# The first mixer's chunk products in diagonal 64x64 tiles, with the whole 64x64 inverse applied during preparation

## The chip, the cores and the metric

The kernel runs on one core of a Trainium2 chip, as one program. The metric is the device time of the program in microseconds (us). Three runs of the kernel before took 3040.48 us in the median (3040.01 to 3050.44). A core has TensorE (PE, matrix products into the accumulator memory PSUM), VectorE (DVE), ScalarE (ACT), GpSimd (POOL) and SyncE (SP, which only issues transfers), and each of these works through its own list of instructions in order.

## The reference

It is one transformer block over 2048 tokens of width 1024: a norm, an input projection `h @ w_in`, two mixers (`hgrn2_mixer`, `rwkv7_mixer`), gates and projections back, and a mixture of experts. The change touches the RWKV mixer, here called the first mixer. For each of its 8 heads it carries a 64x64 state through time:

```
sa = einsum('bhij,bhj->bhi', state, a_t)          # a_t = -kk_t
state = (state * w_t[:, :, None, :] + sa[..., None] * b_t[:, :, None, :]
         + v_t[..., None] * k_t[:, :, None, :])   # b_t = kk_t * a
y_t = einsum('bhij,bhj->bhi', state, r_t)
```

followed by a group norm per head, a bonus term (r * k * r_k summed, times v) and a gate.

## The kernel before, in words

The tokens are worked in 16 blocks of 128 (`TB`), a block in two chunks of 64 tokens. The eight heads lie as four pairs: pair `m` has its two heads on partitions 0 to 63 and 64 to 127.

Inside a chunk the recurrence is solved by products. With the decay taken into the vectors, a chunk needs A and R (`AR`, columns 0 to 63 and 64 to 127), B and K (`BK`), the masked products of these (`Gc`), and U, the solution of a unit triangular system of 64 steps whose right side is A times the state plus a product of `Gc` with the values. Then the state gets B and K times U and the values, and the output is R times the state plus `Gc` times U and the values.

`rw_prep(k, b)` prepares block b without the state. It loads the projected columns (`rwin`, L156), computes tanh, sums, exponentials and the lora products (L173), the norms of the keys (L196, with `iv` as their inverse), the eight products `Gc` in four groups (L224, with L226 as scaling, mask and copy out of PSUM), and sends the 32x32 corners through DRAM (`Nd`) so that all heads' small triangles lie on partitions (`Nl`). A substitution of 31 steps on DVE (L243, L244) inverts each 32x32 triangle; the result goes through DRAM again (`Pd`) and comes back as `Pa` (L251). Transposes give `BT` (L258, L260) and the values `UV` (L268, L272), and the last product is the bonus, `bon` (L279, L280).

`rw_chain(k, b, prep)` runs the two chunks with the state `Sbd` (a 128x128 matrix for each pair, with zeros off the diagonal). Since the inverse is there only for the 32x32 halves, a chunk goes through four dependent steps with a copy on ACT after each: right side of the first half, its solution, the second half's right side, its solution. All its products stand at L296, the one-line helper `mm`. `rw_out` norms, gates and stores a block's output.

What sets the order. The main loop goes over four groups of 512 tokens and issues for each block in turn: the preparation of block b+1, some tiles of input projection, the chain of block b, more projection tiles, the second mixer (`hg_block`), more projection. A planner then orders each engine's list: it takes the instruction that stands earliest in the code among those whose inputs and buffers it expects to be ready, with some blocks of `hg_block` moved forward (`hp`, `HP`). So projection tiles (L770 to L772) fill PE where the mixers wait. From the end of the fourth group on, `mixed` (L853 to L855) takes this place.

Buffers are handed out by name. A name has as many slots as its `bufs`, one where none is given, and the planner gives the slots of a name to its tiles in the order of the code. For this case two names matter: `rp` in PSUM, one slot, through which every product of the preparation goes, and `rwin` in SBUF, one slot.

Of the kernel before, what the change touches and what calls it, by code (L numbers as in the profile page):

```python
# [17 lines left out]
TB = 128  # L18
# [71 lines left out]
def rw_consts(k, I):  # L90
# [4 lines left out]
    k.hind = cp.tile([128, 2], FP, name="hind")  # L95
    nc.gpsimd.memset(k.hind, 0.0)
    nc.gpsimd.memset(k.hind[0:64, 0:1], 1.0)
    nc.gpsimd.memset(k.hind[64:128, 1:2], 1.0)
# [38 lines left out]
    k.iv = [cp.tile([128, TB // 64, 8], FP, name=f"iv{j}") for j in range(2)]  # L137
    for t in k.iv:
        nc.vector.memset(t, 1.0)
    k.Sbd = cp.tile([128, 4, 128], FP, name="Sbd")  # L140
    nc.vector.memset(k.Sbd, 0.0)
# [7 lines left out]
def rw_prep(k, b):  # L149
# [49 lines left out]
    nc.vector.tensor_scalar(iv[0:64], nrm, 1e-24, 2.0, op0=OP.max, op1=OP.mult)  # L199
    nc.vector.reciprocal(iv[0:64], iv[0:64])  # L200
# [17 lines left out]
    for c in range(NC):  # L218
        Gc = w2p.tile([128, 2, 4, 128], FP, name="Gc", bufs=4)
        for hp in range(2):  # L220
            pt = ps.tile([128, 4, 128], FP, name="rp")
            h = slice(hp * 64, hp * 64 + 64)
            for m in range(4):
                nc.tensor.matmul(pt[:, m], BK[h, m, c, :], AR[h, m, c, :], start=(m == 0), stop=True, skip_group_check=True)  # L224
            for m in range(4):
                nc.vector.scalar_tensor_tensor(Gc[:, hp, m], pt[:, m], iv[:, c, 2 * m + hp:2 * m + hp + 1], k.gmask, op0=OP.mult, op1=OP.mult)  # L226
        for hf in range(2):
            q = slice(hf * 32, hf * 32 + 32)
            nc.sync.dma_start(Nd[hf, c * 8:(c + 1) * 8].rearrange("x s t -> s x t"), Gc[q, :, :, q].rearrange("p a m t -> p (a m) t"))
        Gs.append(Gc)  # L230
# [18 lines left out]
    Pa = w2p.tile([64, NC * 8, 32], FP, name="Pa", bufs=2)  # L249
    for hf in range(2):  # L250
        nc.sync.dma_start(Pa[hf * 32:hf * 32 + 32], Pd[hf].rearrange("x s t -> s x t"))  # L251


    BT = []
    for c in range(NC):
        pt = ps.tile([128, 512], FP, name="rp")
        for m in range(4):
            nc.tensor.transpose(pt[:, m * 128:(m + 1) * 128], BK[:, m, c, :], k.ident)  # L258
        t = w2p.tile([128, 4, 128], FP, name="BT", bufs=4)
        nc.vector.tensor_tensor(t.rearrange("p m (h x) -> p (m h) x", h=2), pt.rearrange("p (h x) -> p h x", h=8),  # L260
                                iv[:, c, :, None].to_broadcast([128, 8, 64]), OP.mult)
        BT.append(t)

    UV = []
    for c2 in range(NC // 2):
        pt = ps.tile([128, 512], FP, name="rp")
        for m in range(4):
            nc.tensor.transpose(pt[:, m * 128:(m + 1) * 128], v_[:, m, c2 * 128:(c2 + 1) * 128], k.ident)  # L268
        for j in range(2):
            u = w2p.tile([128, 512], FP, name="UV", bufs=4)  # L270
            nc.gpsimd.memset(u[0:64], 0.0)
            nc.scalar.copy(u[64:128], pt[j * 64:j * 64 + 64])  # L272
            UV.append(u)

# [6 lines left out]
    return AR, Gs, Pa, BT, UV, GE, bon, sY  # L281


def rw_chain(k, b, prep):
# [4 lines left out]
    AR, Gs, Pa, BT, UV, GE, bon, sY = prep  # L289
    Yb = None  # L290
    for c in range(NC):
        Gc, u = Gs[c], UV[c]
        xy = ps.tile([128, 512], FP, name="xy")
        px = ps.tile([128, 512], FP, name="px")
        R = wk.tile([64, 512], FP, name="R")
        mm = lambda *a_, **kw: nc.tensor.matmul(*a_, skip_group_check=True, **kw)  # L296
        hs = [(h, h // 2, h % 2, slice(h * 64, h * 64 + 64)) for h in range(8)]
        for m in range(4):
            mm(xy[:, m * 128:(m + 1) * 128], AR[:, m, c, :], k.Sbd[:, m, :], start=(m == 0), stop=False)
        for h, m, hp, sl in hs:  # L300
            mm(xy[0:64, sl], Gc[:, hp, m, 0:64], u[:, sl], start=False, stop=False)
        nc.scalar.copy(R[0:32], xy[0:32])
        for h, m, hp, sl in hs:
            mm(px[0:32, sl], Pa[0:32, c * 8 + hp * 4 + m, :], R[0:32, sl], start=(h == 0), stop=True)
        nc.scalar.copy(u[0:32], px[0:32])
        for h, m, hp, sl in hs:
            mm(xy[32:64, sl], Gc[0:32, hp, m, 32:64], u[0:32, sl], start=False, stop=False)
        nc.scalar.copy(R[32:64], xy[32:64])
        for h, m, hp, sl in hs:
            mm(px[32:64, sl], Pa[32:64, c * 8 + hp * 4 + m, :], R[32:64, sl], start=(h == 0), stop=True)  # L310
        nc.scalar.copy(u[32:64], px[32:64])
        sp = ps.tile([128, 4, 128], FP, name="px")
        for m in range(4):
# [1206 lines left out]
```

## Time and profile before

| | |
|---|---|
| median of three runs | 3040.48 us |
| the profiled execution | 3035.84 us |
| its span, first to last instruction | 3034.1 us |
| PE busy in the span | 2770.9 us |
| DVE, ACT, POOL busy in the span | 2141.7, 1453.0, 1381.0 us |

The profile is of one execution. An engine's busy time is the time in which at least one of its instructions runs; a matmul is shown from its start to a modelled end, so that neighbours overlap. The mixers run from some 140 us to 1970 us, the experts from about 2200 on.

### The profile page before, as it was taken

The numbers are of one execution on the slowest core, as the hardware profiler recorded it, in microseconds if no ns is written. First come the engines' busy times: TensorE is split into PE (matmuls) and PEld (weight loads), VectorE is DVE, ScalarE is ACT, GpSimd is POOL, SyncE is SP. The second block draws the span as 40 slices with busy tenths as digits, with TensorE's granted clock in tenths as the row PEclk, the third lists the DMA queues.
The fourth block names the chain that finished last, engine by engine and source line by source line (L and its number), as shares of the span: only waits on it lengthen the run. The fifth ranks groups of instructions, "written<-read, shape, count | busy, mean of one in ns | idle before, by whom it ended". The sixth has DMA issues, their size and how long they took to land. (4 is left out here: it accounts for less than half of the span.)

```text
span 3034.1 us, 46921 instructions
## 1 busy us (share of the span) xinstructions
PE 2770.9 (91%) x15562; PEld 2268.7 (75%) x15562; DVE 2141.7 (71%) x4010; ACT 1453.0 (48%) x2507; POOL 1381.0 (46%) x1416
## 2 busy tenths in 40 slices
PE   5999999999999999989999988989987999999993
PEld 5877778778777878778777877868875777777772
DVE  5265787675687667787658778546574698998884
ACT  4334444534444534444434454442233576676763
POOL 3435555655555655565564566663333112221112
PEclk7999999999989999999999998999988999999996
DMA  7565344564444654454453554686456799999996
GB/s 222 161 201 148 100 133 120 151 183 134 105 133 114 181 154 134 113 152 133 131 136 101 150 160 148 203 298 212 152 189 175 260 368 364 363 352 362 361 315 249
DMA packets 569571, 593.16 MB, mean 195 GB/s; under 512 B 113841, under 2 KB 441521, under 8 KB 569218
## 3 DMA queue, kind: packets, MB, share of 16 engines
q1 hardware_dynamic: 556978, 555.11, 57.4%
q0 software_dynamic: 11088, 29.60, 4.2%
q10 hardware_dynamic: 1152, 4.19, 0.4%
q8 instruction: 165, 2.70, 0.4%
q14 instruction: 188, 1.54, 0.2%
HBM read 476.87 MB, written 118.77 MB: 196 GB/s over the span
## 5 line engine op out<-in xcount | busy, mean ns | idle before, releaser
L765 POOL TENSOR_TENSOR wlo<-wraw,whi 128x512 fp32r<-128x512 f32 x368 | 490.9, 1337 | 429.0 <-ACT whi L764 369.4
L770 PE MATMUL mm<-hThi,whi 128*128 128x512 f32 x1472 | 597.3, 406 | 14.8 <-ACT hThi L667 11.9
L772 PE MATMUL mm<-hThi,wlo 128*128 128x512 f32 x1472 | 592.7, 403 | 9.2 <-POOL wlo L765 8.9
L771 PE MATMUL mm<-hTlo,whi 128*128 128x512 f32 x1472 | 592.0, 402 | 1.8 <-DVE hTlo L668 1.8
L1203 DVE TENSOR_TENSOR wlo<-raw,whi 128x1024 fp32r<-128x1024 f32 x404 | 484.1, 1255 | 44.4 <-ACT whi L1202 21.8
L1202 ACT CAST whi<-raw 128x1024 fp32r<-128x1024 f32 x408 | 405.1, 1057 | 209.2 <-PE U L928 51.7
L764 ACT CAST whi<-wraw 128x512 fp32r<-128x512 f32 x368 | 225.9, 616 | 308.6 <-PE mm L771 192.3
L770 PEld LDWEIGHTS mm<-hThi,whi 128*128 128x128 f32 x1472 | 283.2, 192 | 82.3 <-ACT hThi L667 12.4
L772 PEld LDWEIGHTS mm<-hThi,wlo 128*128 128x128 f32 x1472 | 282.4, 192 | 73.0 <-POOL wlo L765 13.8
L771 PEld LDWEIGHTS mm<-hTlo,whi 128*128 128x128 f32 x1472 | 282.9, 192 | 60.7 <-DVE hTlo L668 2.8
L1291 POOL DMA_INDIRECT X<-y,lists x33 | 72.2, 2189 | 489.7 <-DVE y L1289 445.3
L243 DVE TENSOR_TENSOR pr<-Pl,Nl 128x2 f32<-128x2 f32 (+30 forms) x496 | 260.3, 525 | 12.2
L451 POOL TENSOR_TENSOR Xq<-h,kf 128x256 f32<-128x256 f32 x96 | 81.5, 849 | 114.3 <-ACT h L448 71.0
L244 DVE TENSOR_REDUCE Pl<-pr 128x1 f32<-128x2 f32 (+30 forms) x496 | 123.7, 249 | 11.5
L447 ACT ACTIVATE h<-h 128x256 f32<-128x256 f32 x96 | 40.4, 420 | 161.7 <-DVE h L446 158.0
L296 PE MATMUL xy<-UV,Gc 128*64 128x64 f32 (+1 forms) x1536 | 114.6, 224 | 0.0
L1233 PE MATMUL G<-whi,xh 128*128 128x512 f32 x256 | 104.9, 410 | 9.5 <-PEq L1364 8.3
L853 PE MATMUL mm<-hThi,whi 128*128 128x512 f32 x256 | 105.0, 413 | 9.3 <-ACT hThi L667 9.3
L296 PEld LDWEIGHTS xy<-UV,Gc 128*64 128x64 f32 (+1 forms) x1536 | 96.6, 128 | 17.6 <-issue 6.1
L854 PE MATMUL mm<-hTlo,whi 128*128 128x512 f32 x256 | 105.3, 411 | 3.3 <-DVE hTlo L668 3.3
L849 POOL TENSOR_TENSOR wlo<-wraw,whi 128x512 fp32r<-128x512 f32 x64 | 89.0, 1393 | 40.3 <-ACT whi L848 28.5
L226 DVE SCALAR_TENSOR_TENSOR Gc<-rp,iv,gmask 128x128 f32<-128x128 f32 x256 | 71.7, 342 | 46.3 <-PE rp L224 45.8
(492 smaller groups left out, 6184.8 us busy)
## 6 DMA issues: line engine op xcount, KB each, us to landing
wraw<-in_w_in_dram SPq DMA_DIRECT2D x368, 256.0 KB
raw<-in_exp_w_gate_dram SPq DMA_DIRECT2D x126, 512.0 KB
raw<-in_exp_w_up_dram SPq DMA_DIRECT2D x126, 512.0 KB
raw<-in_exp_w_down_dram SPq DMA_DIRECT2D x124, 512.0 KB
HGP<-ev SPq DMA_DIRECT2D x64, 256.0 KB
xin<-in_ada_w_dram SPq DMA_DIRECT2D x32, 512.0 KB
hgin<-HGP SPq DMA_DIRECT2D x16, 1024.0 KB
GTP<-ev SPq DMA_DIRECT2D x64, 256.0 KB
```

The source lines that it names most:

```text
L243: nc.vector.tensor_tensor(pv, Pl[:, :ni, :ns], Nl[:, :ns, t_][:, None, :].to_broadcast([128, ni, ns]), OP.mult)
L244: nc.vector.tensor_reduce(Pl[:, :ni, t_], pv, AX.X, OP.add)
L296: mm = lambda *a_, **kw: nc.tensor.matmul(*a_, skip_group_check=True, **kw)
L764: nc.scalar.copy(whi, raw)
L765: nc.gpsimd.tensor_tensor(wlo, raw, whi.bitcast(FP), OP.subtract)
L770: nc.tensor.matmul(pt, whi[:, kk % 4], hi[kk // 2][:, kk % 2], start=(kk == 0), stop=False)
L771: nc.tensor.matmul(pt, whi[:, kk % 4], lo[kk // 2][:, kk % 2], start=False, stop=False)
L772: nc.tensor.matmul(pt, wlo[:, kk % 4], hi[kk // 2][:, kk % 2], start=False, stop=(kk == 7))
L853: nc.tensor.matmul(pt, whi[:, kk], hi[o // 2][:, o % 2], start=(kk == 0), stop=False)
L854: nc.tensor.matmul(pt, whi[:, kk], lo[o // 2][:, o % 2], start=False, stop=False)
L1202: s.nc.scalar.copy(hi, raw)
L1203: eng.tensor_tensor(lo, raw, hi.bitcast(FP), OP.subtract)
```

## The change

The two heads of a pair get products of their own, on rows and columns 0 to 63 and 64 to 127 of the array, issued in turns. The state becomes `Sst`, 64x64 for each head. The two 32x32 inverses are joined to the whole 64x64 inverse (`PT`) in the preparation, which multiplies A by it (back into `AR`) and the values' part of the right side (into the second half of `UV`). The chain then needs one addition where it had four dependent steps. Transposes become products with a 64x64 identity. Cut to its core:

```diff
@@ rw_prep
-    nrm = pt[0:64, 0, 0:8 * NC].rearrange("p (c h) -> p c h", c=NC)
+    nrm = pt[:, 0, 0:4 * NC].rearrange("p (c m) -> p c m", c=NC)
+    mm = lambda *a_, **kw: nc.tensor.matmul(*a_, skip_group_check=True, **kw)
     for c in range(NC):
         for m in range(4):
-            nc.tensor.matmul(nrm[:, c, 2 * m:2 * m + 2], sq[:, m, c], k.hind, start=(c + m == 0), stop=True,
-                             skip_group_check=True)
+            for h in HEADS:
+                mm(nrm[h, c, m:m + 1], sq[h, m, c], k.ones[h, 0:1], start=(c + m == 0), stop=True)
...
-        for hp in range(2):
+        for w in range(2):
             pt = ps.tile([128, 4, 128], FP, name="rp")
-            h = slice(hp * 64, hp * 64 + 64)
             for m in range(4):
-                nc.tensor.matmul(pt[:, m], BK[h, m, c, :], AR[h, m, c, :], start=(m == 0), stop=True, skip_group_check=True)
+                for h in HEADS:
+                    mm(pt[h, m], BK[h, m, c, w * 64:w * 64 + 64], AR[h, m, c, :], start=(m == 0), stop=True)
+            if w:
+                nc.vector.tensor_tensor(Gc[:, 1], pt, k.gmask[:, None, :].to_broadcast([128, 4, 128]), OP.mult)
+                continue
             for m in range(4):
-                nc.vector.scalar_tensor_tensor(Gc[:, hp, m], pt[:, m], iv[:, c, 2 * m + hp:2 * m + hp + 1], k.gmask, op0=OP.mult, op1=OP.mult)
-        for hf in range(2):
-            q = slice(hf * 32, hf * 32 + 32)
-            nc.sync.dma_start(Nd[hf, c * 8:(c + 1) * 8].rearrange("x s t -> s x t"), Gc[q, :, :, q].rearrange("p a m t -> p (a m) t"))
+                nc.vector.scalar_tensor_tensor(Gc[:, 0, m], pt[:, m], iv[:, c, m:m + 1], k.gmask, op0=OP.mult, op1=OP.mult)
+            for hp in range(2):
+                for hf in range(2):
+                    q = slice(hp * 64 + hf * 32, hp * 64 + hf * 32 + 32)
+                    x = hp * NC * 4 + c * 4
+                    nc.sync.dma_start(Nd[hf, x:x + 4].rearrange("x s t -> s x t"), Gc[q, 0, :, hf * 32:hf * 32 + 32])
...
+    PT = k.PT[b % 2]            # four loads from Pd, two as Pa before
+    for c in range(NC):
+        ab, kv = (ps.tile([128, 512], FP, name="rp") for _ in range(2))
+        for m in range(4):
+            for h in HEADS:
+                mm(ab[h, m * 64:m * 64 + 64], AR[h, m, c, 0:64], k.ident[h, h], start=(m == 0), stop=True)
+        ...                     # B into ab; K and v into kv; copies to at, t and u
+        pt = ps.tile([128, 512], FP, name="rp")
+        for m in range(4):
+            for h in HEADS:
+                mm(pt[h, m * 64:m * 64 + 64], Gs[c][h, 1, m, 0:64], u[h, m * 64:m * 64 + 64], start=(m == 0), stop=True)
+        nc.scalar.copy(u[:, 256:512], pt[:, 0:256])
+    first, second = (tuple(slice(h.start + o, h.start + o + 32) for h in HEADS) for o in (0, 32))
+    P1T = wk.tile([128, NI * 32], FP, name="pr").rearrange("p (x j) -> p x j", j=32)
+    nc.vector.transpose(P1T, PT[:, :, 0:32])
+    pt = ps.tile([128, 512], FP, name="rp")
+    for x in range(NC * 4):
+        for a1, a2 in zip(first, second):
+            mm(off(pt)[a2, x], Gs[x // 4][a1, 0, x % 4, 32:64], P1T[a1, x], start=(x == 0), stop=True)
+    Q = wk.tile([128, NI, 32], FP, name="Pl")
+    for a2 in second:
+        nc.scalar.copy(Q[a2], off(pt)[a2])
+    pt = ps.tile([128, 512], FP, name="rp")
+    ...                         # Q by PT, copied into PT[a1, :, 32:64]
     for c in range(NC):
         pt = ps.tile([128, 512], FP, name="rp")
         for m in range(4):
-            nc.tensor.transpose(pt[:, m * 128:(m + 1) * 128], BK[:, m, c, :], k.ident)
...
+            for h in HEADS:
+                mm(pt[h, m * 64:m * 64 + 64], AT[c][h, m * 64:m * 64 + 64], PT[h, c * 4 + m], start=(m == 0), stop=True)
+        for m in range(4):
+            for h in HEADS:
+                mm(pt[h, 256 + m * 64:320 + m * 64], PT[h, c * 4 + m], UV[c][h, 256 + m * 64:320 + m * 64], start=False, stop=True)
+        nc.scalar.copy(AR[:, :, c, 0:64], pt[:, 0:256].rearrange("p (m t) -> p m t", m=4))
+        nc.scalar.copy(UV[c][:, 256:512], pt[:, 256:512])
     ...                         # bon stands behind this, as before
@@ rw_chain (the old body, L296 to L323, goes)
+        for m, h, lo, hi in ms:
+            mm(x[h, lo], AR[h, m, c, 0:64], S[h, m], start=(m == 0), stop=True)
+        U = wk.tile([128, 256], FP, name="U")
+        nc.vector.tensor_tensor(U, x[:, 0:256], u[:, 256:512], OP.add)
+        for m, h, lo, hi in ms:
+            mm(x[h, hi], AR[h, m, c, 64:128], S[h, m], start=False, stop=False)
+        for m, h, lo, hi in ms:
+            mm(sp[h, lo], bk[h, 4 + m], u[h, lo], start=(m == 0), stop=False)
+        for m, h, lo, hi in ms:
+            mm(sp[h, lo], bk[h, m], U[h, lo], start=False, stop=True)
+        s4 = sp[:, 0:256].rearrange("p (m i) -> p m i", m=4)
+        nc.vector.tensor_tensor(S, s4, S, OP.add)
+        nc.vector.tensor_tensor(S, S, GE[:, :, c:c + 1].to_broadcast([128, 4, 64]), OP.mult)
+        ...                     # x[h, hi] gets Gc by u and by U, 16 products
+        nc.scalar.copy(Yb[:, c * 4:c * 4 + 4], x[:, 256:512].rearrange("p (m i) -> p m i", m=4))
+    rw_out(k, b, 0, Yb, bon, sY)
@@ rw_out
-    for m in range(4):
-        nc.tensor.transpose(pt[:, m], sqf[:, m * 128:(m + 1) * 128], k.ident)
+    for c in range(TB // 64):
+        for m in range(4):
+            for h in HEADS:
+                nc.tensor.matmul(pt[h, m, c * 64:c * 64 + 64], sq[h, c * 4 + m], k.ident[h, h], start=(c + m == 0), stop=True, skip_group_check=True)
```

## Rows read from the trace of the kernel before

**Rows 1.** The page's first part, TensorE: busy us, share, instructions.

```profile
PE 2770.9 (91%) x15562; PEld 2268.7 (75%) x15562; DVE 2141.7 (71%) x4010; ACT 1453.0 (48%) x2507; POOL 1381.0 (46%) x1416
```

**Rows 2.** Windows: stretch, length, each engine's busy us, granted clock, DMA share, GB/s.

```profile
100.00:1990.00 1890.00, 1779.46 (x11013) 1464.65 (x11012) 1321.29 (x2776) 854.84 (x1667) 1067.58 (x1121) 0.97 0.51 145
1600.00:1900.00 300.00, 273.70 (x1738) 227.70 (x1737) 238.18 (x470) 142.18 (x261) 173.67 (x183) 0.93 0.50 141
1900.00:2000.00 100.00, 90.19 (x520) 74.29 (x517) 53.48 (x70) 49.85 (x73) 66.78 (x49) 0.93 0.75 244
```

**Rows 3.** One line's instructions, L160: ns min/median/max, first and last start.

```profile
L160 ACT ACTIVATE rwin<-rwin x16: 308/309/312, 141.6 to 1742.3; 32x128 f32<-32x128 f32 x16
```

**Rows 4.** Window of L296's instructions alone: PE busy, weight loads busy.

```profile
100.00:1990.00 1890.00, 258.68 (x3072) 222.92 (x3072) 0.97 0.51 145
```

**Rows 5.** Groups of PE instructions: count, busy us, mean ns, idle before.

```profile
L224 PE MATMUL rp<-AR,BK 64*128 64x128 f32 x512 | 76.9, 288 | 7.0 <-DVE BK L213 3.7 <-DVE Gc L226 2.1 <-DVE carry L779 1.1
...
L258 PE MATMUL rp<-ident,BK 128*128 128x128 f32 x128 | 20.2, 278 | 1.2 <-DVE Gc L226 1.2
...
L196 PE MATMUL rp<-hind,BK 128*64 128x2 f32 x256 | 19.7, 205 | 1.9 <-ACT BK L190 1.9
```

**Rows 6.** Timeline of PE: start, length, instructions merged, idle before.

```profile
802.22 1.16 PE L224 MATMUL rp<-AR,BK 64*128 64x128 f32 x8
803.30 1.08 PE L296 MATMUL xy<-UV,Gc 32*32 32x64 f32 x16
804.31 0.50 PE L770 MATMUL mm<-hThi,whi 128*128 128x512 f32 x1
```

**Rows 7.** Timeline of the preparation that opens at 1005 us, several engines.

```profile
1005.07 0.31 ACT L160 ACTIVATE rwin<-rwin 32x128 f32<-32x128 f32 x1 [1.42 <-DMA rwin<-RWP]
...
1043.66 1.11 DVE L226 SCALAR_TENSOR_TENSOR Gc<-rp,iv,gmask 128x128 f32<-128x128 f32 x4
1053.50 1.11 DVE L226 SCALAR_TENSOR_TENSOR Gc<-rp,iv,gmask 128x128 f32<-128x128 f32 x4
...
1067.11 0.14 DVE L243 TENSOR_TENSOR pr<-Pl,Nl 128x2 f32<-128x2 f32 x1
...
1074.63 1.16 PE L279 MATMUL rp<-t,rkw 128*128 128x128 f32 x8
...
1077.35 0.68 DVE L280 TENSOR_TENSOR bon<-rp,rwin 128x512 f32<-128x512 f32 x1
1078.06 0.36 SPq L156 DMA_DIRECT2D rwin<-RWP  x1
1084.73 0.31 ACT L160 ACTIVATE rwin<-rwin 32x128 f32<-32x128 f32 x1 [3.20 <-DMA rwin<-RWP]
...
1106.30 0.42 DVE L244 TENSOR_REDUCE Pl<-pr 128x8 f32<-128x256 f32 x1
```

**Rows 8.** Timeline around one return of the inverse from DRAM.

```profile
456.44 0.41 DVE L244 TENSOR_REDUCE Pl<-pr 128x8 f32<-128x256 f32 x1
...
463.93 1.08 PE L296 MATMUL px<-R,Pa 32*32 32x64 f32 x16 [0.74 <-DMA Pa<-Pd]
```

**Rows 9.** Timeline of the preparation that opens at 1208.69, first and last row.

```profile
1208.69 0.31 ACT L160 ACTIVATE rwin<-rwin 32x128 f32<-32x128 f32 x1
...
1339.97 0.41 DVE L244 TENSOR_REDUCE Pl<-pr 128x8 f32<-128x256 f32 x1
```

**Rows 10.** Groups of DVE instructions: the substitution's two lines, all 16 blocks.

```profile
L243 DVE TENSOR_TENSOR pr<-Pl,Nl 128x2 f32<-128x2 f32 (+30 forms) x496 | 260.3, 525 | 12.2
L244 DVE TENSOR_REDUCE Pl<-pr 128x1 f32<-128x2 f32 (+30 forms) x496 | 123.7, 249 | 11.5
```

**Rows 11.** Timeline at the stage's end: last output copy, gate, and the waiting projection.

```profile
1941.81 0.58 ACT L323 COPY Yb<-xy 64x512 f32<-64x512 f32 x1 [1.52 <-PE xy L296]
...
1961.01 0.69 DVE L353 TENSOR_TENSOR Yb<-px,Yb 128x512 f32<-128x512 f32 x1
...
1985.67 0.79 PE L853 MATMUL mm<-hThi,whi 128*128 128x512 f32 x1 [9.34 <-ACT hThi L667]
```

More of the change, by code (lines that the diff above doesn't have):

```diff
@@ L94, in rw_consts @@
     nc.gpsimd.memset(k.rs64[:, :, 0:1], 0.0)
[L95 to L98, printed above, removed]
     def col(name, src):
@@ L136, in rw_consts @@
         nc.vector.tensor_scalar(k.E0[p], e[p], float(rp), None, op0=OP.is_equal)
[L137 to L141, printed above, removed]
+    k.iv = [cp.tile([128, TB // 64, 4], FP, name=f"iv{j}") for j in range(2)]
+    k.PT = [cp.tile([128, TB // 16, 64], FP, name=f"PT{j}") for j in range(2)]
+    for t in k.PT:
+        nc.gpsimd.memset(t, 0.0)
+    k.Sst = cp.tile([128, 4, 64], FP, name="Sst")
+    nc.vector.memset(k.Sst, 0.0)
+HEADS = (slice(0, 64), slice(64, 128))
 def hp(tc, on):
@@ L248, in rw_prep @@
         nc.sync.dma_start(dst[:, rp:32:RQ, :], Pl[rp * NBL:rp * NBL + NBL])
[L249 to L254, printed above, removed]
+    PT = k.PT[b % 2]
+    for hp in range(2):
+        for hf in range(2):
+            q = slice(hp * 64 + hf * 32, hp * 64 + hf * 32 + 32)
+            nc.sync.dma_start(PT[q, :, hf * 32:hf * 32 + 32], Pd[hf, hp * NC * 4:(hp + 1) * NC * 4].rearrange("x s t -> s x t"))
@@ L255, in rw_prep @@
+    Q = wk.tile([128, NI, 32], FP, name="Pl")
+    for a2 in second:
+        nc.scalar.copy(Q[a2], off(pt)[a2])
+    pt = ps.tile([128, 512], FP, name="rp")
+    for x in range(NC * 4):
+        for a1, a2 in zip(first, second):
+            mm(off(pt)[a1, x], Q[a2, x], PT[a2, x, 32:64], start=(x == 0), stop=True)
+    for a1 in first:
+        nc.scalar.copy(PT[a1, :, 32:64], off(pt)[a1])
     for c in range(NC):
@@ L257, in rw_prep @@
         for m in range(4):
-            nc.tensor.transpose(pt[:, m * 128:(m + 1) * 128], BK[:, m, c, :], k.ident)
[L259 to L266, printed above, removed]
-        for m in range(4):
[L268 to L273, printed above, removed]
+            for h in HEADS:
+                mm(pt[h, m * 64:m * 64 + 64], AT[c][h, m * 64:m * 64 + 64], PT[h, c * 4 + m], start=(m == 0), stop=True)
+        for m in range(4):
+            for h in HEADS:
+                mm(pt[h, 256 + m * 64:320 + m * 64], PT[h, c * 4 + m], UV[c][h, 256 + m * 64:320 + m * 64], start=False, stop=True)
+        nc.scalar.copy(AR[:, :, c, 0:64], pt[:, 0:256].rearrange("p (m t) -> p m t", m=4))
+        nc.scalar.copy(UV[c][:, 256:512], pt[:, 256:512])
     nc.gpsimd.tensor_tensor(kp, kp, r_, OP.mult)
@@ L280, in rw_prep @@
     nc.vector.tensor_tensor(bon, pt, v_, OP.mult)
-    return AR, Gs, Pa, BT, UV, GE, bon, sY
+    return AR, Gs, BT, UV, GE, bon, sY
 def rw_chain(k, b, prep):
@@ new lines, in rw_chain @@
+    AR, Gs, BT, UV, GE, bon, sY = prep
+    S = k.Sst
+    mm = lambda *a_, **kw: nc.tensor.matmul(*a_, skip_group_check=True, **kw)
+    ms = [(m, h, slice(m * 64, m * 64 + 64), slice(256 + m * 64, 320 + m * 64)) for m in range(4) for h in HEADS]
+    Yb = wk.tile([128, 8, 64], FP, name="Yb")
+    for c in range(NC):
+        Gc, u, bk = Gs[c], UV[c], BT[c]
+        x = ps.tile([128, 512], FP, name="xy")
+        sp = ps.tile([128, 512], FP, name="px")
+        for m, h, lo, hi in ms:
[11 more added lines that the diff above has]
+        nc.vector.tensor_tensor(S, S, GE[:, :, c:c + 1].to_broadcast([128, 4, 64]), OP.mult)
+        for m, h, lo, hi in ms:
+            mm(x[h, hi], Gc[h, 1, m, 64:128], u[h, lo], start=False, stop=False)
+        for m, h, lo, hi in ms:
+            mm(x[h, hi], Gc[h, 0, m, 64:128], U[h, lo], start=False, stop=True)
+        nc.scalar.copy(Yb[:, c * 4:c * 4 + 4], x[:, 256:512].rearrange("p (m i) -> p m i", m=4))
@@ L341, in rw_out @@
     pt = ps.tile([128, 4, 128], FP, name="px")
-    sqf = sq.rearrange("p h i -> p (h i)")
-    for m in range(4):
-        nc.tensor.transpose(pt[:, m], sqf[:, m * 128:(m + 1) * 128], k.ident)
+    for c in range(TB // 64):
+        for m in range(4):
+            for h in HEADS:
+                nc.tensor.matmul(pt[h, m, c * 64:c * 64 + 64], sq[h, c * 4 + m], k.ident[h, h], start=(c + m == 0), stop=True, skip_group_check=True)
     ob = wk.tile([128, 4, 128], FP, name="Yb")
```

54 lines of the change are left out of this document (17 added, 37 removed).

## The prediction

> **What bounds the kernel now.** I read the page's busy list first: TensorE (PE) is busy 2770.9 us of a span of 3034.1 [rows 1]. Then the windows of the mixer stage: from 100 to 1990 us PE is busy 1779.5 of 1890 us and VectorE (DVE) 1321.3 [rows 2]. So the stage is bound by PE as a whole, and what the mixer does not use of PE, the input projection fills. The slack is in the end of the stage: 26.3 us without PE in 1600 to 1900, 9.8 in 1900 to 2000 [rows 2].
>
> A stage that is full on average can still have a second limit close behind: the pace at which one preparation follows the other. The preparation opens with L160, the first time at 141.6 us, the sixteenth at 1742.3 [rows 3], so a block has (1742.3 - 141.6) / 15 = 106.7 us. The reader should hold every path through one preparation against this number.
>
> **The change, PE's part.** Removed: all products of L296, 258.7 us of busy time [rows 4], and L224, L258 and L196 with 76.9 + 20.2 + 19.7 [rows 5]; two more groups of transposes (values, output), 128 in all, cost some 20 by L258's 0.158 each. Together 396 us. A float32 product is two matmul instructions: L258's transposes are one each, but the 1536 products of L296 show 3072.
>
> Added, counted in the code the same way, for 16 blocks: 7168 matmuls of 64 columns (turned copies 2048, first part of the values 512, A and values through the inverse 1024, chain 3072, output 512), 1024 of 128 columns for G, 1024 of 32x32 in the inverse, 512 of one column for the norms. Prices from the timeline: sixteen 64-column matmuls take 1.08 us, the last of them 0.21, so (1.08 - 0.21) / 15 = 0.058 each; eight of 128 columns take 1.16, the last 0.29, so 0.125 [rows 6]. The norms have L196's 0.077. One after the other that is 7168 x 0.058 + 1024 x 0.125 + 1024 x 0.058 + 512 x 0.077 = 416 + 128 + 59 + 39 = 642 us. Each group's last matmul is seen some 0.16 us longer than its spacing; with 21 groups in a block (1 norms, 4 G, 6 copies and values, 4 inverse, 5 chain, 1 output) that is 336 x 0.16 = 54. So the sum is 696, or 300 us more than now, if a matmul waits for the one of the other head; if the two heads of a pair run fully beside each other, 321 + 54 = 375, or 21 less. No row shows two tiles of the array in turns, so these are the two ends. I take the lower one, since the two heads share neither rows nor columns. Changes of the array's shape cost the same on both sides: after the sixteen the next 128-row matmul starts at 804.31 instead of 803.30 + 16 x 0.058 = 804.23 [rows 6], and the old block leaves that shape about as often.
>
> Two moving columns cost as much as 64: L196 has 2 and still takes 0.077 [rows 5], so something else than the moving columns sets its price. The Trainium skill ("TensorE: Matmul & The Clock Gate", Part 3, The mechanism) says that a weight load overlaps matmuls in flight only where the row groups differ, and the two heads differ in them; by it the sum is the lower end, -21. The same page (LDWEIGHTS) gives a load as columns / 1.2 ns, 53 ns for 64, and loads in turn would give the upper end, +300. No run here shows which.
>
> **The order of the preparation, which I take to decide.** PSUM's name rp has one slot, and the planner gives a name's slots in the order of the code. Now nothing on rp waits for the inverse: `bon` (L279, L280), the last user of rp and the last reader of rwin, runs in the middle of the substitution, and the next load of rwin is issued at its end: 1077.35 + 0.68 = 1078.03, L156 at 1078.06, next L160 at 1084.73 [rows 7]. In the new code two products of the inverse and two of A stand on rp ahead of `bon`, and they need the inverse back from DRAM. So the next block's load, and all its groups on rp, wait for it. What used to lie beside the next preparation comes into the period:
> - From L160 to the third of the four L226 groups: 1043.66 + 1.11 - 1005.07 = 39.7 us. The fourth (1053.50) is no longer needed for the inverse, since the first 128 rows now hold both heads: 9.8 us won.
> - From the fourth to the end of the substitution: 1106.30 + 0.42 - 1054.61 = 52.1 [rows 7].
> - Out to DRAM and back: 463.93 - (456.44 + 0.41) = 7.1 [rows 8].
> - New steps: a DVE transpose of 128x256 (not in the trace; 0.4 to 0.9, I take 0.6), four PE groups of 32 (1.0 to 1.9) and their eight copies (about 0.4, between 0.3 and 0.6), 0.6 + 4 x 1.0 + 4 x 0.8 = 7.8; eight hand-overs at about 1 us behind other work: 16 in all, 10 to 22.
> - `bon`: 1077.35 + 0.68 - 1074.63 = 3.4, load 6.7 [rows 7].
> - Sum 39.7 + 52.1 + 7.1 + 16 + 3.4 + 6.7 = 125 us, against 106.7.
>
> Bounds: the block that opens at 1208.69 has its last substitution step end at 1340.38 [rows 9], 131.7 instead of 101.6: 155 us. Downwards: the substitution itself needs (260.3 + 123.7) / 16 = 24 us of DVE [rows 10] of the 39.6 that it takes here from Nl's arrival; with nothing between, and new steps at 10, it is 103. A late preparation is the oldest work, so less will stand before it: I give back half of that wait, 8 us, and take 117.
>
> **The sum.** Fifteen periods: 15 x (117 - 106.7) = +155. The end gets shorter. Now 1985.67 - 1742.3 = 243.4 us pass from the last L160 to the projection that waits for the last block [rows 3, 11]. New: 39.7 + 52.1 + 7.1 + 16 = 115; two chunks of the chain at some 7 (six groups at 0.5 to 1 us, three DVE steps near 0.5, hand-overs), 14; output as now, 1961.70 - 1941.81 = 19.9; store and load 1985.67 - 1961.70 = 24. That is 173, 70 less. So +155 - 70 = +85: zero is at a period of 111.4. PE's own -21 brings nothing while it waits. From the profiled execution's 3035.84: 3121; the median shown is 4.6 above that execution, so 3125.
>
> **At nothing.** The chain's four 32-row copies of about 0.57 go, and shorter ones of 256 columns come, seven in a chunk: ScalarE is busy half the stage. DVE loses half of L226, L317 and L318 and gets an addition per chunk: less work, and not what ends last. Four more stores and two more loads of the inverse per block are a fraction of a us each on SP's queue (L156's issue took 0.36); behind them stand weight loads four tiles deep. POOL loses the clearing of UV. If DVE's cover went, each new DVE step of some 0.5 us would cost 16 to 32 times that, 8 to 16 us.
>
> **Rivals.**
> - Pairs do not overlap (the pairing does not do what it says): PE's +300 binds, and 106.7 + 300 / 16 = 125 hides the preparation's path. 3340. For it: only one tile position was ever in use at a time. Against: nothing shared.
> - The path fits: a period under 111.4 but PE as full as now, within 15 us, 3040. For it: the low end of 103.
> - The other side: the period stays below 106.7, since hg and fills run ahead and leave DVE free. Then the shorter end counts: of the 36 us without PE in 1600 to 2000 [rows 2] most go, and up to 21 of PE's work; I take 35: 3005. It decides from 34 us instead of 52 between the fourth L226 and the substitution's end (125 - 106.7 = 18 less). Against it: in the block at 1005, at the head of a group, the preparation was already the oldest work.
>
> **How the numbers follow.** Forecast 0.46, pairs without overlap 0.21, the path fits 0.15, faster 0.18. A measurement of this kernel can tell 0.5%, some 15 us. The forecast alone spans periods from 112 to 127, 3050 to 3275. The forecast and the serial rival are slower; 0.02 of the faster case falls within 15 us, and 0.02 of the forecast too: faster 0.16, same 0.19, slower 0.65. The range runs from 3010, which leaves out half of the faster case, to 3320, which leaves out half of the serial one.
>
> **What would show it.** Right: L160 to L160 at 112 to 127 us in all blocks, with no wait at a group's head; PE idle in the stage, waiting for copies of the inverse; the projection done before the last blocks; neighbouring 64x64 matmuls of two heads starting closer than 0.058. Wrong: `bon` still ahead of the inverse's products; periods of 107 with a full PE; or 0.058 between all small matmuls, which is the serial rival.

## The result, and the profile after

The changed kernel takes 3224.4 us (median; 3222.4 to 3227.4) against 3044.4 for the kernel before on the same chip: ratio 1.059, 95% interval 1.057 to 1.062. It is slower, as forecast, but by 180 us instead of 85. Of the runs profiled, the spans are 3220.6 and 3034.1: 186.5 us are to be found.

The page's first and second part (busy time; the span in 40 slices):

```profile
PE 2827.3 (88%) x21194; PEld 2297.5 (71%) x21194; DVE 2095.8 (65%) x3896; ACT 1434.0 (45%) x2601; POOL 1367.5 (42%) x1383
...
PE   6988999899999899998989889649995999999993
...
PEclk9999999999999999999999999769997999999996
```

TensorE is busy 56 us more than in [rows 1] and idle 130 us more (186.5 - 56.4). Inside the mixer stage the slices in which it is least busy, and its clock lowest, are the two around 2100 us, where the stage ends. The mixer's opening line (L162, once L160) and the memset of Nl, which starts a substitution and of which each preparation has one, say how the blocks follow one another:

```profile
L162 ACT ACTIVATE rwin<-rwin x16: 293/309/312, 143.4 to 2064.5; 32x128 f32<-32x128 f32 x16
```

```profile
L244 DVE MEMSET Nl<- x16: 85/85/85, 194.6 to 2097.2; 128x32 f32 x16
```

From opening to opening a block now takes (2064.5 - 143.4) / 15 = 128.1 us instead of the 106.7 of [rows 3]; nine of the fifteen lie between 112 and 127, the others go up to 153.6. The whole difference is then accounted for in three terms: the first opening +1.8, fifteen periods +320, and from the last opening to the end of the span 1156.1 instead of 1291.8, -136. Sum 186.

What is late in a block? The block that opens at 1005.8, on three engines:

```profile
1102.12 0.41 DVE L252 TENSOR_REDUCE Pl<-pr 128x8 f32<-128x256 f32 x1
...
1111.89 0.45 DVE L296 STREAM_TRANSPOSE pr<-PT 128x256 f32<-128x256 f32 x1 [4.66 <-DMA PT<-Pd]
```

```profile
1115.16 0.48 PE L811 MATMUL mm<-hThi,whi 128*128 128x512 f32 x1
...
1116.49 0.69 PE L196 MATMUL rp<-pr,Gc 32*32 32x32 f32 x32
...
1122.80 0.69 PE L196 MATMUL rp<-PT,Pl 32*32 32x32 f32 x32
...
1128.59 0.68 PE L196 MATMUL rp<-PT,AT 64*64 64x64 f32 x16
...
1138.59 0.39 PE L813 MATMUL mm<-hThi,wlo 128*128 128x512 f32 x1
1138.82 1.05 PE L327 MATMUL rp<-t,rkw 128*128 128x128 f32 x8
```

```profile
1117.66 0.74 ACT L304 COPY Pl<-rp 32x256 f32<-32x256 f32 x2
...
1123.54 0.74 ACT L310 COPY PT<-rp 32x256 f32<-32x256 f32 x2 [0.71 <-PE rp L196]
...
1134.12 0.38 ACT L321 COPY UV<-rp 128x256 f32<-128x256 f32 x1
```

The inverse is back at 1111.9, 9.4 after the substitution's end. Its first product starts 4.2 us after the transpose's end, the second 4.4 after Q's copy, A's product 4.3 after the copy into PT, and `bon` 4.3 after the last copy. In each gap TensorE works through projection matmuls (L811 to L813) and other small groups that stand ahead in its queue: it is not idle, it is elsewhere. This block lies at the upper end: over the first fifteen the same four waits are 1.9, 2.7, 3.8 and 3.3 us on the mean. The same steps in the last block, when the projection has run out:

```profile
2125.07 1.07 PE L196 MATMUL rp<-pr,Gc 32*32 32x32 f32 x32 [14.03 <-DVE pr L296]
2126.96 1.06 PE L196 MATMUL rp<-PT,Pl 32*32 32x32 f32 x32 [0.83 <-ACT Pl L304]
2128.86 1.12 PE L196 MATMUL rp<-PT,AT 64*64 64x64 f32 x16 [0.83 <-ACT PT L310]
```

```profile
2126.17 0.74 ACT L304 COPY Pl<-rp 32x256 f32<-32x256 f32 x2 [14.71 <-PE rp L196]
```

Here the next product starts 0.05 us after the copy's end (the 0.83 us of idle time are the two copies, 0.74, and the hand-overs at both their ends), and the join (from the transpose's start to the last copy of A and the values' part) takes 10.4 us instead of 22.6. Of the 130 us that TensorE idles more, 75 lie ahead of the preparation's products and 11 ahead of the chain's and the output's. The longest entries of its waits on rp and px (us, times, longest):

```profile
PE rp L196 <- DVE pr L296: 22.2, 6, 14.0
PE px L385 <- DVE ysq L380: 17.1, 6, 6.1
...
PE rp L196 <- DVE BT L276: 12.7, 8, 3.2
```

I summed TensorE's instructions of the traces by function, as time until an instruction's end or the next one's start, and idle time by the function that starts after it:

| TensorE, us | before | after | E4 | E11 | E13 |
|---|---|---|---|---|---|
| mixer (preparation, chain, output), busy | 411 | 431 | 436 | 438 | 440 |
| projection and mixing, busy | 1270 | 1297 | 1290 | 1276 | 1291 |
| all else, busy | 1090 | 1100 | 1099 | 1107 | 1094 |
| idle ahead of the preparation | 22 | 98 | 87 | 88 | 38 |
| other idle time | 183 | 237 | 216 | 201 | 206 |

(Between its first and its last instruction; E11's join is counted with the mixer.) The new products cost TensorE 20 us more than the old ones. But E4 has the old products, and with some 5 us of added ones they cost 436 there: a lower clock can give the 20 by itself (mean granted clock 0.954 before, 0.939 after, 0.934 in E4).

### The profile page after: what moved, and what is told of

It is laid out like the page before. It is cut to its first block, busy times and chain, and to the rows that moved or that the text cites. A ratio compares the mean times of both kernels' runs of the same rounds, so it can differ in the third digit from the quotient of the medians.

```text
span 3220.6 us, 58431 instructions
## 1 busy us (share of the span) xinstructions
PE 2827.3 (88%) x21194; PEld 2297.5 (71%) x21194; DVE 2095.8 (65%) x3896; ACT 1434.0 (45%) x2601; POOL 1367.5 (42%) x1383
## 5 line engine op out<-in xcount | busy, mean ns | idle before, releaser
L811 PE MATMUL mm<-hThi,whi 128*128 128x512 f32 x1472 | 604.2, 411 | 17.0 <-ACT hThi L708 13.3
L812 PE MATMUL mm<-hTlo,whi 128*128 128x512 f32 x1472 | 601.0, 408 | 2.5 <-DVE hTlo L709 2.5
L813 PE MATMUL mm<-hThi,wlo 128*128 128x512 f32 x1472 | 598.5, 407 | 5.2 <-POOL wlo L806 5.1
L811 PEld LDWEIGHTS mm<-hThi,whi 128*128 128x128 f32 x1472 | 288.1, 196 | 86.5 <-ACT hThi L708 13.8
L813 PEld LDWEIGHTS mm<-hThi,wlo 128*128 128x128 f32 x1472 | 287.2, 195 | 66.7 <-POOL wlo L806 6.5
L251 DVE TENSOR_TENSOR pr<-Pl,Nl 128x2 f32<-128x2 f32 (+30 forms) x496 | 234.8, 473 | 13.2
L895 PE MATMUL mm<-hTlo,whi 128*128 128x512 f32 x256 | 105.3, 411 | 6.8 <-DVE hTlo L709 6.8
L487 DVE TENSOR_TENSOR h<-cum 128x512 f32<-128x512 f32 x96 | 87.7, 913 | 32.3 <-POOL Xq L492 29.8
L896 PE MATMUL mm<-hThi,wlo 128*128 128x512 f32 x256 | 103.4, 407 | 0.0
L818 DVE SCALAR_TENSOR_TENSOR ev<-mm,mu,ev 128x511 f32<-128x511 f32 x56 | 41.8, 746 | 93.2 <-ACT ev L816 93.1
```

The lines of the kernel that those rows point to most:

```text
L251: nc.vector.tensor_tensor(pv, Pl[:, :ni, :ns], Nl[:, :ns, t_][:, None, :].to_broadcast([128, ni, ns]), OP.mult)
L811: nc.tensor.matmul(pt, whi[:, kk % 4], hi[kk // 2][:, kk % 2], start=(kk == 0), stop=False)
L812: nc.tensor.matmul(pt, whi[:, kk % 4], lo[kk // 2][:, kk % 2], start=False, stop=False)
L813: nc.tensor.matmul(pt, wlo[:, kk % 4], hi[kk // 2][:, kk % 2], start=False, stop=(kk == 7))
L895: nc.tensor.matmul(pt, whi[:, kk], lo[o // 2][:, o % 2], start=False, stop=False)
```

## The experiments

All times are medians; the kernel before, measured beside the variants, took 3041 to 3044. "Period" is (last - first start of the Nl memset) / 15: before (1815.2 - 206.0) / 15 = 107.3, after 126.8.

```profile
L236 DVE MEMSET Nl<- x16: 85/85/85, 206.0 to 1815.2; 128x32 f32 x16
```

| run | time | ratio, 95% | period |
|---|---|---|---|
| E1 bon ahead of the inverse's products | 3164.6 | 1.039 to 1.046 | 118.1 |
| E2 join late | 3208.9 | 1.052 to 1.063 | 117.1 |
| E3 heads apart | 3252.7 | 1.068 to 1.075 | 128.8 |
| E4 before, bon waits for the inverse | 3185.0 | 1.044 to 1.051 | 123.2 |
| E5 two slots of rp | 3328.1 | 1.090 to 1.096 | 125.5 |
| E6 before, two slots of rp | 3068.0 | 1.006 to 1.012 | 108.4 |
| E7 E1, BT on ScalarE | 3158.2 | 1.036 to 1.041 | 118.2 |
| E8 E1, values first | 3183.1 | 1.044 to 1.050 | 119.5 |
| E9 preparation planned first | 3209.1 | 1.052 to 1.058 | 126.3 |
| E10 E1, planned first | 3167.4 | 1.039 to 1.045 | 115.6 |
| E11 E2, planned first | 3172.0 | 1.040 to 1.049 | 111.8 |
| E12 E2, BT on ScalarE | 3184.1 | 1.043 to 1.050 | 116.9 |
| E13 before, seven more groups | 3126.0 | 1.021 to 1.029 | 117.2 |
| E14 E11, two slots of rp | 3264.6 | 1.069 to 1.075 | 117.7 |
| E15 E11, other spread of tiles | 3191.0 | 1.044 to 1.050 | 113.5 |
| E16 E11, BT on ScalarE | 3168.0 | 1.037 to 1.043 | 111.0 |
| E17 before, E4 and E13 together | 3202.1 | 1.050 to 1.057 | 123.9 |

**E1: the place of bon.**

```
+    (kp * r, the bon group and its product with v, unchanged)
     first, second = ...            # P1T, the inverse's two products, A, values
-    (kp * r, the bon group and its product with v)
```

> The changed kernel with the product for bon (and the last reading of rwin) moved ahead of the inverse's products; nothing else. Theory (the preparations follow one another on rp and rwin, and the period of 128 us is their path): the next load, 6.6 us, the bon group, 6.1, and the first steps up to the first product on rp, some 4, leave the period. It falls to about 112, by 15 x 16 = 240 us on the path; but TensorE, busy 1829 us between 100 and 2150, then becomes the bound, so the time falls by 100 to 150 only, to 3075 to 3125. Rival (TensorE's additional groups and changes of shape cost the time, not the order): unchanged, 3210 to 3235.

3164.6: 60 us won, the period 118.1. On the mean of the first fifteen blocks the next block opens 18.0 us after the substitution's end instead of 44.1, but from its opening to the third G group it now takes 55.4 instead of 38.8: its groups on rp still stand behind the inverse. The time lies between the two: more than the rival's nothing, less than the theory's 100 to 150.

**E2: the join off the preparation's path.**

```
-    P1T, pt, Q as "pr", "rp", "Pl" in rw_prep
+def rw_join(k, b, prep):           # called just ahead of rw_chain(k, b, prep)
+    P1T, pt, Q as "P1T", "px", "Qs"; the turned A kept in AR[:, :, c, 0:64]
```

> The changed kernel with the whole join behind the inverse (P1T, the two products of the inverse, Q, A and the values' part) taken out of the preparation and put right ahead of its chain, on the chain's PSUM name px, with tiles of its own for P1T and Q, and the turned A kept in AR instead of a tile of its own. The arithmetic is the same. Theory: the preparation's path is what it was in the kernel before, so periods return to 105 to 110 us, and the time to 3000 to 3060. Rival (TensorE's additional work and changes of shape): 3180 to 3230, with TensorE idle as little as in the kernel before. In between (3060 to 3120): the order costs some 130 and TensorE's side the rest.

3208.9: a miss. The period falls by 10 us, as in E1, and the time by 15, with intervals that overlap. Each new block now waits at a group's head for the projection, as in the kernel before, and TensorE idles 105 us ahead of the preparation's products. Its longest waits there:

```profile
PE rp L196 <- DVE BT L275: 36.6, 15, 5.2
PE rp L196 <- DVE Gc L229: 22.8, 10, 7.6
PE rp L196 <- DVE Gc L232: 21.5, 6, 5.5
```

These are not the inverse, but copies out of rp: with the first limit away, a second one is seen right behind it.

**E3: heads apart.**

```
-        for m in range(4):
-            for h in HEADS:
+        for h in HEADS:
+            for m in range(4):
```

> The changed kernel with the two heads one after the other instead of by turns: in each group the loop over the heads outside, the one over m inside. Same products. If the two heads of a pair run beside each other in the changed kernel (33 ns a 64-column product in its trace) and one after the other here (58), TensorE gets 7168 x 0.025 + 1024 x 0.06 + 1024 x 0.04 + 512 x 0.04 = 300 us more, and the time 150 to 320 us more: 3370 to 3540. If the turns are worth nothing: 3210 to 3240.

3252.7, 28 more than the changed kernel; TensorE's busy time 2936 instead of 2827. The turns are worth 109 us of TensorE (one group of 64-column products below, changed kernel first), but most of that was waiting anyway: TensorE's idle time falls by 80, of which 27 lie ahead of the preparation (98 to 71). My 300 was too high; the 32-row groups still took turns in this variant, and sixteen products started 0.050 us apart on the mean, not 0.058: within a head 0.058, but closer where one head follows the other.

```profile
L196 PE MATMUL rp<-UV,Gc 64*64 64x64 f32 x448 | 19.7, 226 | 0.0
```

```profile
L196 PE MATMUL rp<-UV,Gc 64*64 64x64 f32 x448 | 28.8, 231 | 2.5 <-ACT UV L286 2.5
```

**E4: the wait alone, in the kernel before.**

```
+    pt = ps.tile([128, 512], FP, name="rp")
+    nc.tensor.matmul(pt[0:32, 0:64], Pa[0:32, 0, :], Gs[0][0:32, 0, 0, 0:64], ...)
+    dm = wk.tile([32, 64], FP, name="dm")
+    nc.scalar.copy(dm, pt[0:32, 0:64])
     (bon)
```

> The kernel before, with one product of the inverse (32 rows, 64 columns) and one copy of 32 x 64 ahead of bon, on rp: nothing uses its result, but bon, and so the next load and the next products on rp, now stand behind the inverse. TensorE's other work is that of the kernel before. Theory: the period becomes the path, some 50 from L160 to the fourth L226 group at the head of a group, 8.5 to Nl, 36 to 45 for the substitution, 8 for DRAM, 3 for the new group, 6 for bon, 6.6 for the load: 118 to 127 instead of 106.7, so 15 x 11 to 20 = 170 to 300, less up to 100 for a shorter end: 3110 to 3300. Rival (TensorE): 3040 to 3055.

3185.0: +144 with the old products and one tiny group more. TensorE waits 30.5 us at that group (window 100 to 1990; busy, mean, idle before), and the page's TensorE line shows nearly the same work taking 54 us longer, at a mean granted clock of 0.934 for 0.954:

```profile
L276 PE MATMUL rp<-Gc,Pa 32*32 32x64 f32 x28 | 4.7, 255 | 30.5 <-DMA Pa<-Pd 30.5
```

```profile
PE 2825.4 (89%) x15594; PEld 2312.3 (73%) x15594; DVE 2174.6 (68%) x4010; ACT 1457.0 (46%) x2522; POOL 1378.9 (43%) x1416
```

So in the old kernel the order alone is enough for a loss of four fifths of the size.

**E5, E6: a second slot of rp**, in the changed kernel and in the one before.

```
-  name="rp")          name="mm", bufs=3)
+  name="rp", bufs=2)  name="mm", bufs=2)
```

> The changed kernel with two slots of rp instead of one, and two of the projection's mm instead of three (PSUM has no ninth bank). The order in which rp is given is the same, but a group can run while the one before it is still copied out, and the next preparation's first products need not wait for the last group of the one before. TensorE idles 97 us ahead of the preparation's products in the trace of the changed kernel, 22 in the kernel before. Theory (the preparation, 18 groups on one slot instead of 11, loses time at each hand-over): 50 to 70 of these us go, with 10 to 20 of TensorE's lower clock: 3130 to 3170. Rival (the waits are for the inverse alone, which a second slot doesn't bring earlier, and mm loses a slot): 3215 to 3260.

> The kernel before with the same two edits (rp two slots, mm two). Control: what the edits do where the preparation has 11 groups and none of them waits for the inverse. If the hand-overs count only with 18 groups: 3030 to 3070, at most 20 us won, or some lost at mm. If a second slot of rp helps the kernel before as much as the changed one (60 or more): below 2985.

E5 took 3328.1, 104 more than the changed kernel, E6 27 more than before. Neither account of mine has that. In E5 TensorE idles 155 us ahead of the preparation, most of it for copies and DVE steps of the preparation itself; the period hardly moves. But the second slot does shorten the preparation's way: the join takes 16.5 us on the mean instead of 23.3, and in E6 `bon` ends 14.6 us after the last G copy instead of 25.8. What grows is the projection, which gave up a slot of mm: in E5 TensorE waits 31 us for copies out of mm, 2 us in the changed kernel, and the last L811 starts at 2022.3 instead of 1781.6.

```profile
PE mm L811 <- ACT ev L696: 13.7, 7, 5.3
PE mm L811 <- DVE carry L820: 11.4, 5, 3.9
```

Two slots of rp beside three of mm were not run, so what one slot of rp costs by itself stays open.

**E7, E8: what E1 still waits for.** E7 scales BT's first half in four activations `nc.scalar.activation(t[:, m], ab[...], AF.Identity, scale=iv[:, c, m:m + 1])` instead of one DVE product; E8 puts both chunks' kv groups and `bon` ahead of the ab groups.

> The variant with bon ahead of the inverse (3164.6), and in it BT's first half scaled on ScalarE, four activations, instead of one multiplication on VectorE. In that variant TensorE waits 19.3 us for this multiplication, which stands in VectorE's queue among the substitution's 62 steps, and the inverse's and next preparation's groups stand behind it on rp. Theory (hand-overs behind VectorE's substitution are the second limit): period at the substitution's end from 119 to about 114, time 3080 to 3130. Rival (this wait only moves to the next group): 3150 to 3175.

> The variant with bon ahead of the inverse (3164.6), and in it both chunks' turned keys and values and bon ahead of the turned A and B: the last reading of rwin comes four groups earlier, so the next load too. Products and groups are the same. Theory (rwin's release sets when the next preparation opens): it opens 10 to 20 us earlier, but its first products still stand on rp behind the groups of A, of B and of the inverse; 3110 to 3160. Rival (rp alone sets the pace, so nothing is won): 3155 to 3180.

E7 3158.2, 6 less than E1 and within its uncertainty; the wait moved to the next copy. E8 3183.1, 19 more: the next block opens 3.7 us ahead of the substitution's end, 21.7 earlier than in E1, but takes 75.2 us to its third G group instead of 55.4. Opening earlier wins nothing while the first products stand on rp behind the block before. Both are the rivals' outcomes.

**E9, E10, E11: order of planning.** `HP = [16,16,12]` becomes `[0,16,12]` in the changed kernel, in E1 and in E2.

> The changed kernel with the preparation planned ahead of all other ready work in every block (first entry of HP 0 instead of 16); the work is the same. In the changed kernel the join behind the inverse (P1T to the last copy of A and the values' part) takes 23.3 us in a block beside projection and other mixer, 10.4 in the last block alone, while the substitution and the other terms of the period stay within 2 us of the forecast. Theory (the period's excess over the forecast is hand-overs standing behind other work in the engines' queues): the join falls towards 13 to 16, the period from 128 to 112 to 118, the time to 3060 to 3150. Rival (the hand-overs cost what they cost, or other work that is put back comes late): 3200 to 3260.

> The variant with bon ahead of the inverse (3164.6) with the same edit to HP. Theory: period at the substitution's end from 119 to 105 to 110; TensorE is then the bound, with what it idles at the hand-overs: 3080 to 3140. Rival: 3150 to 3200.

> The variant with the join put ahead of its chain (3208.9) with the same edit to HP. There the inverse is off the preparation's path already, and TensorE is the bound, idle for 105 us ahead of the preparation's products, whose copies stand in VectorE's and ScalarE's queues. If those copies then come earlier: 3120 to 3180. If TensorE, which takes its instructions in their planned order, only reaches the preparation's products sooner and waits as long: 3195 to 3250.

E9 3209.1: the join still takes 23.0 us on the mean, the period 126.3. So the hand-overs are not long because older work is preferred: a late preparation already was the oldest, and still other work stands between. The list is fixed before the program runs; whether a planner that expects the copies to end earlier would put less between is not tested. E10 3167.4, as its rival. E11 3172.0: 37 us less than E2.

**E12, E15, E16: attempts on E2 and E11.** E12 and E16 put BT's scaling on ScalarE as E7 does, E15 spreads the tiles as WS = [[4,5,5],[4,6,6],[2,3,3],[2,3,3]].

> The variant with the join put ahead of its chain (3208.9), BT's first half scaled on ScalarE in four activations instead of on VectorE. TensorE waits 36.6 us for that multiplication in that variant, the longest entry of its waits. Theory: most of these and some of the lower clock behind them are won, 3160 to 3185. Rival (the wait moves to the next copy in line): 3195 to 3220.

> The same variant (3172.0) with the projection's tiles spread differently over a block (WS 4,5,5 and 4,6,6 and 2,3,3 instead of 0,7,7 and 0,8,8 and 0,4,4), so that some stand ahead of the join and the chain; the sums are the same. Theory (the spread was right for a long chain and a short preparation, and isn't for 113 us of chain and 280 of preparation): 3120 to 3160. Rival (the spread hardly matters where TensorE waits on copies): 3160 to 3190.

> The same variant (3172.0) with BT's first half scaled on ScalarE, which won 25 us in the variant without the edit to HP (3208.9 to 3184.1). If the two gains add up: 3135 to 3160. If TensorE's waits only move to the next copy: 3165 to 3185. Faster than the kernel before (3040) in neither case.

E12 won 25 us, E16 nothing beyond the noise; E15 took 19 more, outside both of its accounts, with an interval that overlaps that of E11. No variant comes near the kernel before.

**E13: seven more hand-overs, in the kernel before.**

```
+    for j in range(7):
+        pt = ps.tile([128, 512], FP, name="rp")
+        nc.tensor.matmul(pt[:, 0:64], k.ident, BK[:, j % 4, j % 2, 0:64], ...)
+        dm = wk.tile([128, 64], FP, name="dm")
+        nc.scalar.copy(dm, pt[:, 0:64])
     (bon)
```

> The kernel before with seven more groups on rp in each preparation, ahead of bon: each one product of 128 rows and 64 columns and one copy of 128x64 on ScalarE, that nothing uses and that wait for nothing of the inverse. So the preparation has 18 groups on rp, as the changed kernel has; TensorE gets 112 products, some 25 us. Theory (seven more hand-overs on one slot cost the changed kernel TensorE's idle time also where the inverse is off the path): some 2 us each in the period, or TensorE idle ahead of the preparation's products 60 us more than the 22 of before: 3095 to 3200. Rival (hand-overs are covered by the projection's work): 3035 to 3070.

3126.0: +82 for 112 products that nothing waits for but the next user of rp. That next user is `bon`, so `bon` and the load behind it are later too. The period goes to 117.2, TensorE's idle time up by 38 us, only 15 of it ahead of the preparation where I expected 60, and its busy time by 54, of which the new products are a part.

```profile
L236 DVE MEMSET Nl<- x16: 85/85/85, 207.7 to 1965.6; 128x32 f32 x16
```

**E14: a second slot with the inverse off rp.** The edits of E5 in E11.

> The variant with the join ahead of its chain and the preparation planned first (3172.0), with two slots of rp and two of mm. In the kernel before the same two edits cost 27. Theory (here, with the inverse off rp, the preparation's hand-overs on one slot are what is left): 40 to 60 us of TensorE's idle time go, less those 27: 3130 to 3165. Rival (a second slot brings nothing, the waits are on the copies' place in VectorE's and ScalarE's queues): 3185 to 3260.

3264.6, 93 more than E11: the rival's side, and worse than it said. As in E5 the second slot shortens the preparation (from the third G copy to the end of `bon` 28.4 us instead of 49.2), while the projection takes longer: TensorE waits 27 us for copies out of mm, 3 in E11, and the last L819 starts at 1967.7 instead of 1883.9.

**E17: both additions in the kernel before.**

> The kernel before with both additions: seven more groups on rp in each preparation (+82 alone) and one product of the inverse ahead of bon (+144 alone). TensorE's other work stays that of the kernel before: old products, old chain. Theory (the changed kernel's order and number of hand-overs on rp account for all of its +180, and its new products as such for next to nothing): the two add up, less some 40 where the end of the stage gets shorter with each longer period: 3190 to 3270, with a period near the changed kernel's 128. Rival (the seven groups run beside the substitution, which the wait for the inverse covers already): no more than the wait alone, 3170 to 3190; then some 40 of the +180 are left to the new products.

3202.1: +160, of the changed kernel's +180, with the old products and the old chain. The two additions hide part of each other (144 + 82 = 226). The remaining 20 are not taken apart further; differences of this size came from rearrangements that change no work, too (E6, E8, E15).

```profile
L236 DVE MEMSET Nl<- x16: 85/85/85, 207.3 to 2065.8; 128x32 f32 x16
```

## Why the prediction was right in its direction and wrong in its size

**The decider was right.** The next preparation stands behind the inverse on rp and rwin; E4 shows that this is enough to make the old kernel 144 us slower, E1 that moving `bon` ahead of the inverse, which frees rwin but not rp, gives 60 back. The two rivals with a period under 111.4 are out by the measured 128.1, the serial one by what follows.

**TensorE was near the lower end.** The two heads run beside each other: sixteen products take 0.68 us, the last 0.22, so 0.031 each where [rows 6] had 0.058:

```profile
1001.45 0.68 PE L339 MATMUL xy<-Sst,AR 64*64 64x64 f32 x16
```

The rule of the Trainium skill ("TensorE: Matmul & The Clock Gate", Part 3, The mechanism) that loads overlap where the row groups differ agrees with this. Busy time of the mixer came out at +20 instead of -21. Half of these 41 us the clock can explain (E4's old products: some 431); the rest was not taken apart. E3 shows that little hung on it: 109 us of TensorE were worth 28.

**The step that failed is the new period: "new steps ... 16 in all, 10 to 22".** Means over the first fifteen blocks, from the starts and ends of the same lines:

| term, us | forecast | measured |
|---|---|---|
| L162 to the third G group | 39.7 | 38.8 |
| to the substitution's end (52.1, less the 8 given back) | 44.1 | 45.2 |
| out to DRAM and back | 7.1 | 8.0 |
| join: transpose, four groups, copies | 16 | 23.3 |
| bon, from the last copy's end | 3.4 | 6.2 |
| load | 6.7 | 6.6 |
| sum | 117 | 128.1 |

The 8 us that I gave back were right. What was too cheap is the hand-over: I had eight at about 1 us "behind other work". On an idle TensorE one takes 0.05 us, as the last block shows; with the projection in the queue the three in the join that lead to TensorE take 1.9, 2.7 and 3.8 us on the mean, the two from the inverse's products to their copies 1.9 and 1.1, and the one to `bon` 3.3. Ten of the eleven missing us are the join and `bon`, 15 x 10 = 150. The forecast had the right row in hand for it: in [rows 7] the fourth L226 starts 8.7 us after the third has ended, two hand-overs in a full queue, and I used it only to count what is saved.

**The end of the stage was mis-sized the other way**, -147 instead of -70: from the last opening to the waiting projection it takes 2161.05 - 2064.5 = 96.6 us instead of 243.4. The experts behind it take 11 us more (1059.5 instead of 1048.4), which I had at nothing; -136 is both. I priced the last block at a full block's prices, 115 us from opening to the last copy; alone it took 70 (2064.5 to 2134.8). Chain, output, store and load I had at 58 (14 + 19.9 + 24), the last two from [rows 11], where projection work ran between; here the waiting projection starts 26 us after that last copy:

```profile
2161.05 0.80 PE L894 MATMUL mm<-hThi,whi 128*128 128x512 f32 x1 [8.07 <-ACT hThi L708]
```

The errors, +165 in the periods and -66 behind the last opening, with the first opening's +1.8, leave the 101 between the forecast's 85 and the spans' 186. That the second took back part of the first is luck.

**Not in the forecast: the number of groups on rp.** I counted 21 groups in a block and put 0.16 us of TensorE's time on each; what each waits until rp is free again I did not price. The traces have it, as means of the first fifteen blocks, in the stretch from the last G copy that the inverse needs to the end of `bon`:

| | groups on rp | us | `bon`'s end, from the substitution's end |
|---|---|---|---|
| before | 4 | 25.8 | 27.6 ahead |
| E13 | 11 | 55.7 | 9.6 behind |
| E2 | 8 | 49.0 | 8.1 behind |
| E11 | 8 | 49.2 | 6.7 behind |

So a group costs 5 to 6.5 us here, and more of them push `bon` behind the substitution without any wait for the inverse. The next load waits for `bon`: in E13 the next block opens 16.6 us after the substitution's end, in the kernel before 13.4 ahead of it. One block of E13, against [rows 7]:

```profile
836.89 0.41 DVE L244 TENSOR_REDUCE Pl<-pr 128x8 f32<-128x256 f32 x1
...
853.80 0.68 DVE L285 TENSOR_TENSOR bon<-rp,rwin 128x512 f32<-128x512 f32 x1
```

E13's 82 us thus go with the same change as E4's 144: what lay beside the next preparation comes into the period. E2 and E11 show the same without the inverse on rp: `bon` still ends behind the substitution. That leaves open why E11, with a period of 112, is 130 slower than the kernel before: TensorE idles 88 us ahead of the preparation there. That these 130 are the more numerous copies is argued from the waits, not shown: a copy on another engine (E16) did not bring them back, and E14 gave rp a second slot only by taking one from mm. The Trainium skill has the general rule ("TensorEngine Tiling (Array Packing)", PSUM Bottleneck): tiling speeds up TensorE, not the emptying of PSUM, whose copies may become the bottleneck after a fourfold speed-up. The trace goes that way with two heads at a time: busy time of the mixer about as before, wait ahead of the preparation 98 us for 22.

**The clock** was lower too, and what it cost of the 186 us was not separated: from 100 to 1990 us TensorE had 0.97 [rows 2], now 0.95, and at the stage's end less, after the projection had run out and TensorE had stood idle:

```profile
100.00:1990.00 1890.00, 1730.60 (x15302) 1404.36 (x15301) 1190.29 (x2461) 795.89 (x1676) 1013.87 (x1055) 0.95 0.49 137
...
2100.00:2200.00 100.00, 58.04 (x606) 48.42 (x603) 45.57 (x84) 30.51 (x47) 29.11 (x16) 0.73 0.48 162
```

0.73 is a mean of the two levels; the 32x32 products there take 1.07 us a group, 0.69 in mid-stage.

## What to carry to other kernels

Price a hand-over by the queue it goes through: here 0.05 us on an idle engine, 2 to 4 on the mean where another stage kept it full; a chain of eight then cost more than the arithmetic that it saved. Count the groups on a resource with one slot as well: at 5 to 6.5 us each they set when its last user, and with it the next block, can start. Before putting work that needs a late-known value (here the inverse) on a resource with one slot, look which later work stands behind that slot, and test it in the old kernel with one dummy product: E4 cost a few lines and showed four fifths of the result. A control that changes two things (here a slot of rp for one of mm) answers neither. When a limit is lifted and the time stays, look for the next one right behind it, and price the last block of a stage by itself, since little stands in its way.

## What the runs showed of the hardware

Two heads' 64x64 products in the two diagonal quarters of the array, both writing the same PSUM tile in different partitions, started 0.031 us apart on the mean, by turns 0.007 and 0.052, against 0.058 for the products of one head in a row (E3). A slower multiplication was seen on VectorE now and then: `L251` on 256 columns took over 1.1 us in three of the sixteen blocks (1.22 in the first row) and 0.59 in the last.

```profile
1100.32 1.22 DVE L251 TENSOR_TENSOR pr<-Pl,Nl 128x256 f32<-128x256 f32 x1
...
2116.56 0.59 DVE L251 TENSOR_TENSOR pr<-Pl,Nl 128x256 f32<-128x256 f32 x1
```

What shares the time with it is not settled by these runs.
